# A hybrid attention encoder on one core: the last dilated merge over later slots, the first head's loads and splits reordered, the copies of branch B's values moved into dilated slots

## The chip, the cores and the metric

The kernel runs on one core of one Trainium2 chip. The metric is the device time of one execution in microseconds (us), the median of several runs. Five engines work side by side, each through its own queue in order: TensorE (PE in the profile, PEld for its weight loads), VectorE (DVE), ScalarE (ACT), GpSimd (POOL) and SyncE (SP), which here only issues DMAs.

## The reference

One encoder layer on 1024 positions of width 1024, in float32. What matters here is the attention part, which has two branches on the same normalised input `h`:

```python
proj = h @ w_in
qa, ka, va, qb, kb, vb, ga, gb = split(proj)
oa = mixture_of_dilations(qa, ka, va, rel_bias)      # branch A, 8 heads of 64
ob = neighbourhood_attention_2d(qb, kb, vb, na_rpb)  # branch B, 8 heads of 64
merged = sigmoid(ga) * (oa @ w_branch_dil) + sigmoid(gb) * (ob @ w_branch_na)
x = x + gate1 * (merged @ w_out)
```

Branch A runs three dilated window patterns and merges them per position with weights from their softmax denominators. Branch B is attention over an 8 x 16 neighbourhood on a 16 x 64 grid. A convolutional FFN and a final norm follow.

## The kernel before, in words

Each float32 product is three TensorE products of rounded parts: every operand is split into a high part (an ACT copy into a rounded type) and a low part (a subtraction on POOL or DVE), and high x high, high x low and low x high are summed in PSUM. So each weight tile costs one ACT step and one or two POOL steps before TensorE can use it.

**Stages.** First come the norm and the conditioning, then the values of both branches (`v_wide`), then the queries and keys (`p_products`, the "p stage", lines 500 to 521 and 795 to 850), then attention (lines 852 to 1400), then the branch and output products and the FFN. In the p stage a pair of weight tiles is loaded by `p_load` (L714) and split by `a_operands` (L442 to L461 and the helper's L57 and L61). In this stage a scheduler orders every engine's queue when the kernel is built, from its own estimates of time.

**The copies of branch B's values.** `v_wide` writes vB to `vbc` in DRAM. Four column blocks of it are copied, DRAM to DRAM, to the tensors `vb` from which the heads load (`vb_chunks`, L423, 16 DMAs in all). They are written in the p stage's loop (L829), but the scheduler puts them as early in SP's queue as it finds them ready.

**Attention in slots.** Attention is written as a table: slot 0 to slot 101, and in each slot lists of jobs ("first", "O", "T", "S", "last"). `settle` (L898) opens a slot: it emits the ACT and DVE work that the slot before left. Then come "first", "O" (probabilities times values), "T" (transposes of the probabilities), one step of fill work, "S" (scores) and "last", and one or two more fill steps. Fill work is the gate projection: each step is a triple of 128x512 products (L84 to L86). Small jobs such as splits wait in a side queue (`aside`) and are emitted with the fill steps; `ensure` emits what is not out yet. This order is fixed by hand for PE, ACT, DVE and SP. **POOL's order in attention is not**: the scheduler sets it at build time, by when it believes each step to be ready.

- Dilated heads (`DilHead`): head n starts at slot 8n. It adds a bias part on POOL (L1008), makes `qb` on POOL (L408), splits its values `vv` (ACT L780, POOL L781), and runs scores, softmax (DVE L882, ACT L883), transposes (L1039, L1087), their splits into `th` (ACT L892) and `tl` (DVE L896), and outputs (L1051, L1104).
- Dilated pairs (`DilPair`): two heads share tiles `u1`, `u23`. Their merge is a chain: `spread` reads the denominators back (9 small DMAs), `factors` and `shares` work out the weights on DVE and ACT, `send` writes them to DRAM (`fcs`, 10 DMAs), `load` reads them back broadcast (`fb`, L1183), `weigh` multiplies on POOL (L1188, four times), `merge` adds on POOL (L1197). For the last pair (pr 3, first slot 48) these stand at slots 68 to 81, among the first 2-D heads.
- 2-D heads (`NaHead`): head n starts at slot 64 + 4n. Four column blocks are scored (L1252), softmaxed (DVE L1262, ACT L1264), normalised (reciprocal L1269 on DVE, then one half on POOL and one on DVE, L1272), transposed (L1281) and multiplied (L1294). The values `vv` come by L774 at slot s0 + 2 and are split in three parts (L780, L781).

**The first head** has no slots ahead of it. Its loads, and those that were put beside them (bias and keys of head 1), are issued before the slots start (L854 to L859 and L909), and weight tile 26 of the gate projection is loaded by the fill steps (L1338).

Of the kernel before, what the change touches and what calls it, by code (L numbers as in the profile page):

```python
# [29 lines left out]
def hybrid_encoder(tc, xT, c, w_ada, small, w_in, p1_bias, p23_bias, na_bias, ln2_mult, ident, w_br, w_out,  # L30
# [43 lines left out]
    ahead = {}  # L74
# [320 lines left out]
    def qk_load(head):  # L395
        pr, i = divmod(head, 2)
        a = slice(64 * i, 64 * i + 64)
        qk = [qk2.tile([128, S], FR, name=n) for n in ("qs", "ks", "kl")]
        for y in range(3):
            rows = f(qk[y]).rearrange("(p b) s -> b p s", b=2)  # L400
            for b in range(2):
                sp.dma_start(rows[b], q_scr[pr, 1 + y if y else b, a])
        return qk
# [13 lines left out]
        for j, t0 in ((0, 0), (8, 240)):  # L417
            sp.dma_start(va_b[j, 0:64, cc].rearrange("(r p) n -> r p n", r=4), v4[:, t0:t0 + 16])

    def vb_chunks(cb):  # L420
        t0, n = NA_T0[cb], NA_NC[cb]
        for r in range(4):
            sp.dma_start(vb_s[cb].rearrange("(w t r) n -> r w t n", r=4, t=n)[r],  # L423
                         vb_c[256 * r:256 * r + 256].rearrange("(w t) n -> w t n", t=16)[:, t0:t0 + n])

    STEPS = (("11", "B11"), ("S2", "T2"), ("S1", "T1"), ("S3", "T3"), ("12", "B21"), ("S4", "B22"), ("22", "T4"))
    names = tuple(b for _, b in STEPS)
# [97 lines left out]
    with tc.manual_schedule(engines={e.engine for e in (sp, act, dve, pool, pe)}):  # L525
# [53 lines left out]
        for q in range(4):  # L579
# [16 lines left out]
            last = 6 if q else 5  # L596
# [88 lines left out]
        def v_raw(load, head):  # L685
            vv = sm_pool.tile([128, 16, 128], FR, name="vv", bufs=2)
            load(head, f(vv[:, :, 64:128]))
            return vv

        def dil_bias(head):  # L690
            bt = sm_pool.tile([128, 896], FT, name="bias", bufs=4)
            sp.dma_start(bt[:, 0:512], p1_bias[head])
            sp.dma_start(bt[:, 512:896], p23_bias[head])
            return bt
# [131 lines left out]
    for n in range(len(order)):  # L826
        if n + 2 < len(order):
            raw[n + 2] = p_load(n + 2)
        if 1 <= n < 5:  # L829
            vb_chunks(n - 1)  # L830
        if n + 1 < len(order):
            nxt = prep[1] if n == 0 else a_operands(raw.pop(n + 1), 4, p_home, p_sts[n + 1], spot=p_spot)
            if n:
                next(nxt)
        else:
            ahead.update({t: w_load(w_in[t]) for t in (24, 25)})
            nxt = iter(())
        for j in gens[n] if n < 2 else p_products(n):
            if j in (1, 2, 5):
                next(nxt, None)  # L840
# [12 lines left out]
    with tc.manual_schedule(engines={pool.engine}):  # L853
        qks = {0: qk_load(0)}  # L854
        lnm = sm_pool.tile([128, 384], FT, name="lnm", bufs=1)
        sp.dma_start(lnm, ln2_mult)
        biases = {0: dil_bias(0)}
        values = {0: v_raw(va_load, 0)}
        biases[1] = dil_bias(1)  # L859
        pool.tensor_tensor(biases[0][:, 512:896], biases[0][:, 512:896], lnm, OP.add)  # L860
        q_blocks(qks[0])

# [43 lines left out]
        turned.clear()  # L906
        scored.clear()

    qks[1] = qk_load(1)  # L909
    side, second, count, credit = collections.deque(), collections.deque(), [0, 0], [0]  # L910

    def aside(ns, one=lambda: None, two=lambda: None):
# [64 lines left out]
    class DilHead:  # L977
        def __init__(self, pair, pr, i, s0, u, st):
            self.pair = pair
            self.pr, self.i, self.u, self.st, self.head = pr, i, u, st, 2 * pr + i  # L980
            self.a = slice(64 * i, 64 * i + 64)
            self.P, self.tt, self.po = {}, {}, {}
            if self.head > 1:
                at(s0 - 5, "first", self.load)
                at(s0 - 7, "first", lambda: qks.update({self.head: qk_load(self.head)}))
            if self.head:
                at(s0 - 3, "first", self.load_v)
                at(s0 - 2, "first", self.prepare)
                at(s0 - 1, "first", lambda: q_blocks(qks[self.head]))
            at(s0, "first", self.values)  # L990
            for n in range(4):
                at(s0 + n, "S", self.far_scores, n)
                at(s0 + n + 2, "T", self.far_turn, n)
                at(s0 + n + 4, "O", self.far_out, n)
                at(s0 + n + 4, "S", self.near_scores, n)
                for js in (((0, 1),), ((2, 3),), ((4, 5),), ((6, 7), (8,)))[n]:
                    at(s0 + n + 6 + (js == (8,)), "T", self.near_turn, js)
                    at(s0 + n + 8 + (js == (8,)), "O", self.near_out, js)
# [10 lines left out]

        def values(self):  # L1010
            self.bt, self.vv = biases.pop(self.head), values.pop(self.head)
            for n in range(0, 16, 8):
                self.mark = aside(600, lambda n=n: v_tile(self.vv, ((128, slice(n, n + 8)),)))

# [96 lines left out]
    class DilPair:  # L1111
        def __init__(self, pr):
            self.pr, s0 = pr, 16 * pr
            at(s0, "first", self.begin) if pr else self.begin()
            for i in range(2):
                DilHead(self, pr, i, s0 + 8 * i, lambda: self.u, lambda: self.st)
            at(s0 + 17, "T", self.turn)
            at(s0 + 20, "first", self.spread)
            at(s0 + 22, "last", self.factors)
            at(s0 + 23, "last", self.shares)  # L1120
            at(s0 + 24, "first", self.send)
            for z in range(2):
                at(s0 + 26, "first", self.load, 1, z)
            for n, g, z in ((28, 1, 0), (29, 1, 1), (31, 0, 0), (32, 0, 1)):
                at(s0 + n, "last", self.weigh, g, z)
            at(s0 + 33, "first", self.merge)

        def begin(self):
            self.u = [at_pool.tile([128, S], FT, name=n) for n in ("u1", "u23")]
# [72 lines left out]
    class NaHead:  # L1202
        def __init__(self, head, s0):
            self.head, self.i = head, head % 2
            self.a = slice(64 * self.i, 64 * self.i + 64)
            self.P, self.t3, self.bt = {}, {}, {}
            at(57 if head == 0 else s0 - 4, "first", lambda: qks.update({8 + head: qk_load(8 + head)}))
            at(s0, "first", self.begin)
            at(s0 + 2, "first", self.load)
            at(s0 + 4, "last", self.prepare)  # L1210
            for n, cb in enumerate((0, 3, 1, 2)):
                at(s0 + n - 2, "first", self.bias, cb)
                at(s0 + n, "S", self.scores, cb)
                at(s0 + n + 2, "first", self.normalise, cb)
            for n, pair in enumerate(((0, 3), (1, 2))):
                s = s0 + 4 + 2 * n
                for y in range(3):
                    at(s + (y == 2), "T", self.turn, pair, y)
                at(s + 3, "O", self.out, pair)
# [1 line left out]
        def begin(self):  # L1221
            self.st = at_pool.tile([128, 2, 8], FT, name="stb", bufs=3)

        def load(self):
            if self.i == 0:
                oTs[self.head // 2] = (gspool.tile([128, S], FT, name="last", bufs=1) if self.head == 6 else
                                       at_pool.tile([128, S], FT, name=("u1", "u23")[self.head // 2 % 2]))
            self.vv = v_raw(vb_load, self.head)

        def prepare(self):  # L1230
# [81 lines left out]
    def fill_steps():  # L1312
        w, raw = first_w, {1: ahead.pop(25)}
        w_mark = 0
        marks, held = [0, 0], []

        def out(p, n, hf):
            g = gspool.tile([128, 512], FT, name="gs")
            act.activation(g, p, AF.Copy)
            if now[0] < LAST:  # L1320
                later(1, lambda: sp.dma_start(g_scr[n][:, halves[hf]], g))
            else:
                act.dma_start(g_scr[n][:, halves[hf]], g)

        def release():
            while held:
                args = held.pop()
                marks.append(aside(600, lambda: out(*args)))
        for n in range(16):
            ensure(w_mark)  # L1330
            if n < 15:
                w_next = [wpool.tile([128, KT, 128], FR, name=x_) for x_ in ("whi", "wlo")]
                w_mark = side_split(raw.pop(n + 1), *w_next)
            if n < 14:
                raw[n + 2] = w_load(w_in[26 + n])
            elif n == 14:
                w_raw[0] = w_load(w_br[0])
            for hf in range(2):  # L1338
                ensure(marks[2 * n + hf])
                p = ps_g.tile([128, 512], FT, name="pj")  # L1340
                for k in range(KT):
                    product(p, w, lambda k: h[hf, k], ks=[k])
                    if k == 1:
                        release()
                    if k == KT - 1:
                        held.append((p, n, hf))
                        if n == 15 and hf:
                            release()
                    yield
            w = w_next  # L1350
# [3 lines left out]
        DilPair(pr)  # L1354
    for head in range(8):
        NaHead(head, 64 + 4 * head)
    steps = fill_steps()

    def fill(n, asides=True):
# [758 lines left out]
```

## Time and profile before

| What | Value |
|---|---|
| Time, median of 3 runs | 1481.3 us (1480.17 to 1482.05) |
| The profiled execution | 1483.17 us, of which the span from first to last instruction is 1481.3 us |
| PE busy | 1448.3 us, 98% of the span |
| POOL, DVE, ACT busy | 58%, 64%, 53% of the span |
| PE's granted clock, mean | 0.994 of full speed |

The page gives shares of a span that has stages with quite different limits. TensorE is busy nearly throughout, so what is left to win or lose lies in short places where it waits, or where its clock is lower; these are read from the windows (busy time and granted clock by stretch) and from the timeline, which gives the idle time ahead of an instruction in brackets with what ended it.

### The profile page before, as it was taken

Reading aid. Unit: us, or ns where it says so; the run is one execution under the profiler, and the core shown is the slowest. Engines: PE = TensorE matmul, PEld = TensorE weight load, DVE = VectorE, ACT = ScalarE, POOL = GpSimd, SP = SyncE. Lnnn points to the kernel's source line nnn. Section 1 sums busy time; section 2 is a strip of 40 time slices with the busy share of each in tenths; the row PEclk is TensorE's granted clock in tenths of the full one; section 3 lists DMA queues with packets and bytes.
Section 4 is the critical chain, followed back from the end, with each engine's and each line's share of the span. In section 5 each row is a group of like instructions: output and inputs, shape, how many; then the busy total and the mean of one; then the engine's idle time right before and its main releaser. Section 6 shows DMA issues by size and latency. Waiting matters only on the chain.

```text
span 1481.3 us, 21309 instructions
## 1 busy us (share of the span) xinstructions
PE 1448.3 (98%) x7308; PEld 1224.1 (83%) x7308; DVE 952.1 (64%) x1793; ACT 792.3 (53%) x1479; POOL 858.5 (58%) x706
## 2 busy tenths in 40 slices
PE   9999999999999989999999999999999999999998
PEld 8887788788888878888888878888888888887787
DVE  7696544255555756666516897666666667787865
ACT  6634543277777657653346554444444447475542
POOL 4155775434554566512267678766666676988712
PEclk9999999999999999999999999999999999999999
DMA  9598354654765788477644313222222233542313
GB/s 368 206 349 293 124 185 178 216 156 138 209 189 169 228 259 276 146 271 255 196 155 138 108 52 134 85 86 86 86 85 82 69 132 128 199 149 65 110 37 114
DMA packets 130516, 241.14 MB, mean 163 GB/s; under 512 B 47812, under 2 KB 60740, under 8 KB 130372
## 3 DMA queue, kind: packets, MB, share of 16 engines
q1 hardware_dynamic: 121176, 219.00, 45.2%
q10 hardware_dynamic: 9232, 20.78, 3.8%
q8 instruction: 58, 0.95, 0.3%
q14 instruction: 50, 0.41, 0.1%
HBM read 185.60 MB, written 59.90 MB: 166 GB/s over the span
## 4 chain that ended last, share of the span: by engine, by line
PE 76%; DVE 7%; DMA 5%; POOL 4%; ACT 3%; issue 3%; SPq 1%; ACTq 0%; DVEq 0%; POOLq 0%
PE pj L496 14%; PE pj L497 14%; PE pj L498 14%; PE pj L84 8%; PE pj L85 7%; PE pj L86 7%; PE O L1294 1%; PE O L1104 1%; PE O L1051 1%; PE T L1039 1%; PE T L1281 1%; PE T L1087 1%; DVE op L1648 1%; PE S L1252 1%; POOL wlo L61 1%
## 5 line engine op out<-in xcount | busy, mean ns | idle before, releaser
L61 POOL TENSOR_TENSOR wlo<-wraw,whi 128x512 fp32r<-128x512 f32 (+1 forms) x90 | 114.1, 1289 | 129.3 <-ACT whi L57 127.5
L496 PE MATMUL pj<-op,wsh 128*128 128x512 f32 x408 | 158.7, 390 | 1.6 <-ACT wsh L57 1.6
L497 PE MATMUL pj<-op,wsh 128*128 128x512 f32 x408 | 158.9, 390 | 0.5 <-DVE op L1537 0.5
L498 PE MATMUL pj<-op,wsl 128*128 128x512 f32 x408 | 157.6, 390 | 0.0
L61 POOL TENSOR_TENSOR wsl<-big,wsh 128x512 fp32r<-128x512 f32 (+1 forms) x86 | 111.7, 1321 | 44.4 <-ACT wsh L57 39.4
L84 PE MATMUL pj<-h,whi 128*128 128x512 f32 x272 | 116.8, 430 | 0.0
L86 PE MATMUL pj<-h,wlo 128*128 128x512 f32 x272 | 107.7, 396 | 0.0
L85 PE MATMUL pj<-h,whi 128*128 128x512 f32 x272 | 107.7, 396 | 0.0
L1747 DVE SCALAR_TENSOR_TENSOR big<-pj,sm,big 128x512 f32<-128x512 f32 (+2 forms) x183 | 94.9, 563 | 16.5 <-ACT big L1741 15.5
L882 DVE CUSTOM_DVE_ANT_0 P<-S,bias 128x256 f32<-128x256 f32 x128 | 49.1, 421 | 68.2 <-PE S L1024 39.5
L496 PEld LDWEIGHTS pj<-op,wsh 128*128 128x128 f32 x408 | 76.6, 188 | 18.3 <-ACT wsh L57 2.5
L496 PE MATMUL pj<-op,whi 128*128 128x512 f32 x232 | 90.8, 391 | 0.3 <-ACT wc L502 0.3
L497 PE MATMUL pj<-op,whi 128*128 128x512 f32 x232 | 90.6, 391 | 0.2 <-DVE op L1567 0.2
L497 PEld LDWEIGHTS pj<-op,wsh 128*128 128x128 f32 x408 | 76.6, 188 | 16.8 <-DVE op L1537 0.9
L498 PE MATMUL pj<-op,wlo 128*128 128x512 f32 x232 | 90.4, 390 | 0.0
L61 POOL TENSOR_TENSOR wsl<-wraw,wsh 128x384 fp32r<-128x384 f32 (+1 forms) x46 | 56.7, 1254 | 57.3 <-ACT wsh L57 53.0
L498 PEld LDWEIGHTS pj<-op,wsl 128*128 128x128 f32 x408 | 76.7, 188 | 15.9 <-POOL wsl L61 0.2
L883 ACT ACTIVATE P<-P,st 128x256 f32<-128x256 f32 x128 | 64.0, 502 | 38.2 <-DVE st L882 37.9
L896 DVE TENSOR_TENSOR tl<-T,th 128x512 fp32r<-128x512 f32 (+3 forms) x120 | 76.0, 648 | 11.5 <-ACT th L892 11.5
L57 ACT ACTIVATE whi<-wraw 128x1024 fp32r<-128x1024 f32 (+2 forms) x48 | 47.5, 993 | 58.3 <-PE pj L85 33.5
L1741 ACT ACTIVATE big<-pj,sm 128x512 f32<-128x512 f32 x61 | 47.0, 773 | 54.2 <-DVE pj L517 32.2
L517 DVE TENSOR_TENSOR pj<-pj,wc 128x512 f32<-128x512 f32 x40 | 27.8, 695 | 71.9 <-PE pj L498 71.9
(478 smaller groups left out, 4566.0 us busy)
## 6 DMA issues: line engine op xcount, KB each, us to landing
wada<-w_ada SPq DMA_DIRECT2D x31, 512.0 KB
qks<-qs ACTq DMA_DIRECT2D x28, 512.0 KB
wraw<-w_in SPq DMA_DIRECT2D x24, 512.0 KB
big<-w_up SPq DMA_DIRECT2D x22, 512.0 KB
wraw<-w_up SPq DMA_DIRECT2D x22, 512.0 KB
big<-as SPq DMA_DIRECT2D x22, 512.0 KB
as<-big SPq DMA_DIRECT2D x21, 512.0 KB
qs<-qks SPq DMA_DIRECT2D x32, 256.0 KB
```

What stands on the lines that cost most here:

```text
L57: act.activation(hi, raw, AF.Copy)
L61: lo_eng.tensor_tensor(lo[:, i:i + step], raw[:, i:i + step], f(hi)[:, i:i + step], OP.subtract)
L84: pe.matmul(psum, whi[:, k0 + k], mhi, start=k == 0, stop=False)
L85: pe.matmul(psum, whi[:, k0 + k], mlo, start=False, stop=False)
L86: pe.matmul(psum, wlo[:, k0 + k], mhi, start=False, stop=k == n - 1)
L496: pe.matmul(psum, whi[:, k], bhi, start=j < 4 and k == 0, stop=False, skip_group_check=True)
L497: pe.matmul(psum, whi[:, k], blo, start=False, stop=False, skip_group_check=True)
L498: pe.matmul(psum, wlo[:, k], bhi, start=False, stop=k == n - 1, skip_group_check=True)
L882: dve.tensor_tensor_reduce(pp, d, bias, -1.0, BIG, OP.add, OP.min, mi)
L883: act.activation(pp, pp, AF.Exp, bias=mi, scale=-1.0, accum_out=li)
L896: dve.tensor_tensor(tt[1][:m, :n], pt[:m, :n], f(tt[0])[:m, :n], OP.subtract)
L1747: dve.scalar_tensor_tensor(y[:, dst], src, wt, y[:, dst], OP.mult, OP.add)
```

## The change

Four edits, all of them in which order work is issued; no arithmetic changes.

1. The 16 copies of vB are no longer written in the p stage. Each is a job of its own at slots 10, 12, ... 40.
2. The first head: weight tile 26 is loaded ahead of the first head's values. The bias and the keys of head 1 are no longer loaded before the slots start but by head 1's own jobs (slots 3 and 1). The splits of head 0's values, which were emitted in slot 0, are emitted in slot 2.
3. The last pair's merge steps move from slots 68, 70, 71, 72, 74, 76, 77, 79, 80, 81 to 70, 72, 73, 74, 76, 79, 80, 83, 84, 85.
4. A 2-D head's values are split from slot s0 + 5 "first" on (it was s0 + 4 "last"), and its output tile is taken at s0 + 6 (it was s0 + 2).

```diff
-    def vb_chunks(cb):
+    def vb_chunk(cb, r):
         t0, n = NA_T0[cb], NA_NC[cb]
-        for r in range(4):
-            sp.dma_start(vb_s[cb]..., vb_c[256 * r:256 * r + 256]...)
+        sp.dma_start(vb_s[cb]..., vb_c[256 * r:256 * r + 256]...)
...
-        if 1 <= n < 5:
-            vb_chunks(n - 1)
...
         biases = {0: dil_bias(0)}
+        ahead[26] = w_load(w_in[26])
         values = {0: v_raw(va_load, 0)}
-        biases[1] = dil_bias(1)
...
-    qks[1] = qk_load(1)
...
-            if self.head > 1:
+            if self.head:
                 at(s0 - 5, "first", self.load)
                 at(s0 - 7, "first", lambda: qks.update({self.head: qk_load(self.head)}))
...
             at(s0, "first", self.values)
+            at(s0 if self.head else 2, "first", self.split_values)
...
-            at(s0 + 20, "first", self.spread)
...
+            steps = (22, 24, 25, 26, 28, (31, 32, 35, 36), 37) if pr == 3 else (20, 22, 23, 24, 26, (28, 29, 31, 32), 33)
+            at(s0 + steps[0], "first", self.spread)
...
-            at(s0 + 4, "last", self.prepare)
+            at(s0 + 6, "first", self.output)
+            at(s0 + 5, "first", self.prepare)
...
-                raw[n + 2] = w_load(w_in[26 + n])
+                raw[n + 2] = ahead.pop(26) if n == 0 else w_load(w_in[26 + n])
...
+    for n in range(16):
+        at(10 + 2 * n, "last", vb_chunk, (0, 3, 1, 2)[n // 4], n % 4)
```

Three places show what this does to the queues. Line numbers of the changed kernel differ a little: L423 is L422, L714 is L713, L780 and L781 are L779 and L780, L883 is L880, L892 is L889, L956 and L957 are L952 and L953, L1272 is L1275, L1319 is L1322.

The first is SP's queue at the start of the p stage. `wraw` and `xr` are weight tiles, `vb<-vbc` the copies. Before:

```order
L423 DMA vb<-vbc 96x1x512
L423 DMA vb<-vbc 128x1x512 x2
L423 DMA vb<-vbc 96x1x512
L714 DMA wraw<-w_in 128x1024 x2
L423 DMA vb<-vbc 96x1x512
L423 DMA vb<-vbc 128x1x512 x2
L423 DMA vb<-vbc 96x1x512
L316 DMA vbc<-vs 128x512
L423 DMA vb<-vbc 96x1x512
L423 DMA vb<-vbc 128x1x512
L714 DMA xr<-w_in 128x1024 x2
```

And with the change, from the same place:

```order
L713 DMA wraw<-w_in 128x1024 x2
L316 DMA vbc<-vs 128x512
L713 DMA xr<-w_in 128x1024 x2
L316 DMA vbc<-vs 128x512
L713 DMA xr<-w_in 128x1024 x2
```

Ten copies that stood ahead of the first two `xr` loads are gone from there. The scheduler has reordered TensorE's queue in this stage too: between the first product with the new tile's high part and the first with its low part `wlo` there stood 18 products with `op` and `kl`, and there stand 9 now.

The second is ACT's queue at the start of the slots. `vv` is the split of head 0's values, `P,st` the exponentials, `th` the split of a transpose, `whi<-wraw` the split of tile 26. Before:

```order
L1319 ACTIVATE gs<-pj 128x512
L780 ACTIVATE vv<-vv 128x8x64 x2
L883 ACTIVATE P,st<-P,st 128x256 x4
L956 ACTIVATE whi<-wraw 128x512
L892 ACTIVATE th<-T 128x512
```

With the change:

```order
L1322 ACTIVATE gs<-pj 128x512
L880 ACTIVATE P,st<-P,st 128x256 x4
L779 ACTIVATE vv<-vv 128x8x64 x2
L889 ACTIVATE th<-T 128x512
L880 ACTIVATE P,st<-P,st 128x256 x2
L952 ACTIVATE whi<-wraw 128x512 x2
```

The first exponentials stand ahead of the value splits, and the first `th` stands ahead of the split of tile 26.

The third is POOL's queue around the first two `weigh` steps of the last pair (`u<-u,fb`). `P<-P,stb` is a half of a normalisation, `vv` the low part of a value split. Before:

```order
L1272 TENSOR_SCALAR P<-P,stb 128x288
L957 TENSOR_TENSOR wlo<-wraw,whi 128x512 x2
L1188 TENSOR_TENSOR u_4512<-u_4512,fb 128x512
L1272 TENSOR_SCALAR P<-P,stb 128x288
L1188 TENSOR_TENSOR u_4512<-u_4512,fb 128x512
L1272 TENSOR_SCALAR P<-P,stb 128x384
L781 TENSOR_TENSOR vv<-vv 96x4x64
```

With the change:

```order
L1275 TENSOR_SCALAR P<-P,stb 128x288 x2
L953 TENSOR_TENSOR wlo<-wraw,whi 128x512 x2
L1275 TENSOR_SCALAR P<-P,stb 128x384
L1188 TENSOR_TENSOR u_4512<-u_4512,fb 128x512 x2
L780 TENSOR_TENSOR vv<-vv 96x4x64
L1275 TENSOR_SCALAR P<-P,stb 128x384
```

Two normalisations of the 2-D head that starts at slot 72 now stand ahead of the `weigh` steps (those of slots 75 and 76), and both `weigh` steps stand in a row ahead of its last one (slot 77).

More of the change, by code (lines that the diff above doesn't have):

```diff
@@ L418, in va_chunks @@
             sp.dma_start(va_b[j, 0:64, cc].rearrange("(r p) n -> r p n", r=4), v4[:, t0:t0 + 16])
-    def vb_chunks(cb):
+    def vb_chunk(cb, r):
         t0, n = NA_T0[cb], NA_NC[cb]
-        for r in range(4):
-            sp.dma_start(vb_s[cb].rearrange("(w t r) n -> r w t n", r=4, t=n)[r],
-                         vb_c[256 * r:256 * r + 256].rearrange("(w t) n -> w t n", t=16)[:, t0:t0 + n])
+        sp.dma_start(vb_s[cb].rearrange("(w t r) n -> r w t n", r=4, t=n)[r],
+                     vb_c[256 * r:256 * r + 256].rearrange("(w t) n -> w t n", t=16)[:, t0:t0 + n])
     STEPS = (("11", "B11"), ("S2", "T2"), ("S1", "T1"), ("S3", "T3"), ("12", "B21"), ("S4", "B22"), ("22", "T4"))
@@ L1011, in values, with split_values @@
             self.bt, self.vv = biases.pop(self.head), values.pop(self.head)
+        def split_values(self):
             for n in range(0, 16, 8):
@@ L1117, in __init__ @@
             at(s0 + 17, "T", self.turn)
-            at(s0 + 20, "first", self.spread)
-            at(s0 + 22, "last", self.factors)
-            at(s0 + 23, "last", self.shares)
-            at(s0 + 24, "first", self.send)
+            steps = (22, 24, 25, 26, 28, (31, 32, 35, 36), 37) if pr == 3 else (20, 22, 23, 24, 26, (28, 29, 31, 32), 33)
+            at(s0 + steps[0], "first", self.spread)
+            at(s0 + steps[1], "last", self.factors)
+            at(s0 + steps[2], "last", self.shares)
+            at(s0 + steps[3], "first", self.send)
             for z in range(2):
-                at(s0 + 26, "first", self.load, 1, z)
-            for n, g, z in ((28, 1, 0), (29, 1, 1), (31, 0, 0), (32, 0, 1)):
+                at(s0 + steps[4], "first", self.load, 1, z)
+            for n, g, z in zip(steps[5], (1, 1, 0, 0), (0, 1, 0, 1)):
                 at(s0 + n, "last", self.weigh, g, z)
-            at(s0 + 33, "first", self.merge)
+            at(s0 + steps[6], "first", self.merge)
         def begin(self):
@@ L1222, in begin, with output @@
             self.st = at_pool.tile([128, 2, 8], FT, name="stb", bufs=3)
-        def load(self):
+        def output(self):
             if self.i == 0:
@@ L1227, in load @@
                                        at_pool.tile([128, S], FT, name=("u1", "u23")[self.head // 2 % 2]))
+        def load(self):
             self.vv = v_raw(vb_load, self.head)
```

## The prediction

> **What bounds the kernel now.** I read the page first. TensorE is busy for nearly the whole span and no other engine passes two thirds of it:
>
> ```profile
> span 1481.3 us, 21309 instructions
> PE 1448.3 (98%) x7308; PEld 1224.1 (83%) x7308; DVE 952.1 (64%) x1793; ACT 792.3 (53%) x1479; POOL 858.5 (58%) x706
> ```
>
> TensorE's work is the same before and after the change, so only its idle time (33 us in all) and the time that it loses at a lower clock can move. Next the windows, which give by stretch the busy time of PE, PEld, DVE, ACT and POOL, the granted clock, the share of DMA and GB/s. Of the stretches that the change touches, three have PE idle, and a fourth, which the copies enter, has not:
>
> ```profile
> 125.00:150.00 25.00, 23.28 (x108) 18.37 (x106) 17.19 (x27) 16.43 (x30) 7.63 (x7) 1.00 0.84 279
> 275.00:300.00 25.00, 20.44 (x102) 16.48 (x101) 6.36 (x21) 7.51 (x20) 13.19 (x14) 1.00 0.81 257
> 525.00:550.00 25.00, 20.25 (x112) 17.78 (x111) 12.50 (x39) 13.66 (x36) 14.64 (x14) 0.86 0.90 274
> 300.00:425.00 125.00, 124.25 (x784) 110.41 (x783) 71.77 (x243) 94.31 (x260) 54.66 (x51) 0.99 0.55 161
> ```
>
> The first is the start of the p stage, the second the start of attention, the third slots 74 to 79. In each I then read the timeline of PE and of the engine that it waits for.
>
> **Edit 1, at the start of the p stage.** TensorE waits twice for the first new weight tile, first for its high part and then for its low part:
>
> ```profile
> 144.76 0.50 PE L496 MATMUL pj<-h,whi 128*128 128x512 f32 x1 [1.31 <-ACT whi L57]
> 145.33 0.40 PE L496 MATMUL pj<-op,kl 128*128 128x512 f32 x1
> 149.20 0.39 PE L498 MATMUL pj<-op,kl 128*128 128x512 f32 x1
> 151.27 0.50 PE L498 MATMUL pj<-h,wlo 128*128 128x512 f32 x1 [1.68 <-POOL wlo L61]
> ```
> ```profile
> 131.11 2.66 SPq L423 DMA_DIRECT2D vb<-vbc  x4
> 136.70 0.33 SPq L316 DMA_DIRECT2D vbc<-vs  x1
> 138.42 1.01 SPq L714 DMA_DIRECT2D xr<-w_in  x2
> 143.65 1.06 ACT L57 ACTIVATE whi<-xr 128x1024 fp32r<-128x1024 f32 x1 [1.29 <-DMA xr<-w_in]
> 146.08 1.29 POOL L442 TENSOR_TENSOR ks<-xr 128x512 f32<-128x512 f32 x1 [17.21 <-DMA xr<-w_in]
> 149.95 2.51 POOL L61 TENSOR_TENSOR wlo<-xr,whi 128x512 fp32r<-128x512 f32 x2
> ```
>
> Both together are 1.31 + 1.68 = 2.99 us. The first `xr` landed 143.65 − 138.42 = 5.2 us after its issue, the second 7.7, while the copies kept the DMA engines at a share of 0.84; then POOL needs 5.1 us from the second landing to the end of the first `wlo` step (146.08 to 149.95 + 1.25). Without copies `xr` is issued right behind `vbc<-vs`, at some 137.1, 1.3 us earlier, and I take the shorter 5.2 us for both: landed at about 142.4, `wlo` ready at 147.5. The wait for `whi` is gone by this. But TensorE also comes earlier: without the first wait it starts at 143.45, does two products with `whi` (0.57 us), and then has 9 products with `op`, `kl` in place of 18, each (149.20 − 145.33)/17 = 0.228 us. So it wants `wlo` at 143.45 + 0.57 + 2.05 = 146.1 and waits 1.4. Gain 2.99 − 1.4 = about 1.5; ends 0 (a landing 1.5 us later than I take it) and 3.0 (all of it).
>
> The Trainium skill, "DMA: Bandwidth & Descriptors", section "Anatomy of one DMA — SWDGE (gpsimd) path", fits 2.0 us plus the bytes over 436 kB/us; for 512 KB that is an estimate of 3.2 us, against the 5.2 and 7.7 us of these rows, and by it the gain would be the full 3.0. The rows decide, since other transfers still share the engines.
>
> The 16 copies come back at slots 10 to 40, one in every second slot. Four issues take SP 2.66 us, so each 0.67. In the fourth window above DMA is busy by 0.55 and PE idles only 0.75 us in 125. The loads of a head stand 5 to 7 slots ahead of its use, and that distance is the cover. I take 0 and weigh the contrary below.
>
> **Edit 2, at the start of attention.** The first transposes wait for the exponentials (L883), the first outputs for `th` (L892), and two stretches behind run at a lower clock:
>
> ```profile
> 290.35 0.33 PE L1039 MATMUL T<-idt,P 128*128 128x128 f32 x1 [1.56 <-ACT P L883]
> 298.78 0.36 PE L1051 MATMUL O<-th,vv 128*128 128x256 f32 x1 [2.55 <-ACT th L892]
> ```
> ```profile
> 287.19 0.42 DVE L882 CUSTOM_DVE_ANT_0 P<-S,bias 128x256 f32<-128x256 f32 x1 [7.50 <-POOL bias L860]
> 289.18 0.63 ACT L780 ACTIVATE vv<-vv 128x512 fp32r<-128x512 f32 x1 [0.96 <-DMA vv<-v]
> 290.39 2.52 POOL L781 TENSOR_TENSOR vv<-vv 128x512 fp32r<-128x512 f32 x2
> 291.74 0.33 SPq L65 DMA_DIRECT2D wraw<-w_in  x1
> 297.52 0.63 ACT L956 ACTIVATE whi<-wraw 128x512 fp32r<-128x512 f32 x1 [5.75 <-DMA wraw<-w_in]
> 298.06 0.58 ACT L892 ACTIVATE th<-T 128x512 fp32r<-128x512 f32 x1
> ```
> ```profile
> 300.00:302.00 2.00, 2.00 (x10) 1.71 (x8) 0.73 (x3) 2.00 (x8) 1.28 (x1) 0.52 0.27 82
> 302.00:304.00 2.00, 2.00 (x11) 1.83 (x10) 0.66 (x3) 0.76 (x3) 0.00 (x0) 0.63 0.92 225
> ```
>
> ACT's queue explains both waits. The exponentials stand behind the `vv` splits, which wait for their load; `th` stands behind the split of tile 26, which was issued at 291.74 and landed 5.8 us later. The idle time is 25.00 − 20.44 = 4.56 us of the second window; at the clocks 0.52 and 0.63 two stretches of 2 us lose 0.96 + 0.74 = 1.70 us of full-speed work. In all 6.26. With the change the exponentials need only DVE's 287.19 + 0.42, and take until about 288.8, where the transposes are wanted (290.35 − 1.56): a wait of some 0.2 stays. Tile 26, issued ahead of `vv`, is there long before its split. What is late next is `vv`: 512 KB more stand ahead of it, at the 257 GB/s of that window 2 us, so it comes at 289.6 to 291.2, and ACT's two `vv` splits (0.63 each) end by 291.8, `th` at 292.4; the `vv` low parts on POOL (2.52) end at about 294.4, when the outputs are due (296.2 less the 1.56 that is gone, so about 294.7). That is just in time. Gain 6.0; ends 6.3 and, if the outputs wait for `vv`, 3.
>
> The Trainium skill, "TensorE: Matmul & The Clock Gate", section "Part 1: The HAM clock gate (the "warmup" mystery)", says that the clock halves after an idle window of about 3.4 us. By it a wait of 2.55 us would keep the clock and edit 2 would win 1.7 less; the rows above show 0.52 of full speed behind just this wait, so I count the 1.7.
>
> **Edit 3, in the 2-D slots.** At slot 76 TensorE's second transposes wait 4.41 us for a normalisation on POOL, which stands behind a `weigh` (L1188) that waits for `fb`:
>
> ```profile
> 523.42 0.60 PE L1281 MATMUL T<-idt,P 128*128 128x128 f32 x4
> ...
> 531.99 0.60 PE L1281 MATMUL T<-idt,P 128*96 128x128 f32 x4
> 537.00 1.09 PE L1281 MATMUL T<-idt,P 128*96 128x128 f32 x4 [4.41 <-POOL P L1272]
> 546.03 0.60 PE L1281 MATMUL T<-idt,P 128*128 128x128 f32 x4
> ```
> ```profile
> 469.39 2.53 SPq L1183 DMA_DIRECT2D fb<-fcs  x4
> 526.16 2.57 SPq L1183 DMA_DIRECT2D fb<-fcs  x4
> 475.56 1.30 POOL L1188 TENSOR_TENSOR u<-u,fb 128x512 f32<-128x512 f32 x1 [8.46 <-DMA fb<-fcs]
> 534.70 1.26 POOL L1188 TENSOR_TENSOR u<-u,fb 128x512 f32<-128x512 f32 x1 [6.64 <-DMA fb<-fcs]
> 538.16 1.24 POOL L1272 TENSOR_SCALAR P<-P,stb 128x384 f32<-128x384 f32 x1
> 623.87 0.72 POOL L781 TENSOR_TENSOR vv<-vv 96x256 fp32r<-96x256 f32 x1
> ```
> ```profile
> 537.00:540.00 3.00, 3.00 (x11) 2.68 (x12) 0.02 (x1) 1.59 (x3) 3.00 (x3) 0.50 1.03 379
> 540.00:543.00 3.00, 3.00 (x15) 2.71 (x14) 2.96 (x8) 1.45 (x5) 2.32 (x4) 0.60 1.02 362
> ```
>
> Two stretches of 3 us at 0.50 and 0.60 lose 1.5 + 1.2 = 2.7, so the place costs 4.41 + 2.7 = 7.1 us. With the change the first two `weigh` steps stand ahead of a part of the `vv` split and of the normalisation of slot 77, for which the second transposes of slot 78 wait. From the first transposes of slot 76 to these are 546.03 − 531.99 − 7.1 + 0.4 = 7.3 us (0.4 for slot 78's first four, which overlap their successors). Before them POOL must do two `weigh` (1.26 to 1.30 each), the split (0.72) and the normalisation (1.24): 4.6 with issue. So `fb` may take 7.3 − 4.6 = 2.7 us counted from slot 76. From issue to first `weigh` it takes 6.2 us in the row of 469 and 8.5 in that of 526. With the change no group of `qs`, `ks`, `kl` and no weight tile stands right ahead of it in SP's queue, only `vv` and two `bias`, so I take somewhat less than the shorter row, 5.7. `fb` is asked for in slot 76 at the earliest place, and SP, which was 2.7 us behind the first transposes of slot 74 (523.42 to 526.16) right after issuing ten `fcs`, now has one slot more behind these, so it should be about 1 us ahead of PE. The wait is then 5.7 − 1 − 2.7 = 2.0 us, which I count without a loss of clock (1.68 us left it at 1.00 in the first stretch, 2.55 halved it in the second). The last two `weigh` steps, one slot apart, may cost 0.5. Gain 7.1 − 2.0 − 0.5 = about 4.5; upper end 7.1, lower end under the first rival.
>
> **Edit 4** puts the splits one job later and the output tile four slots later. The order has one visible cost: the third part of the last head's split comes out only when its output needs it, which can show its POOL step (0.72); I take 0.5 lost.
>
> **Sum:** 1.5 + 6.0 + 4.5 − 0.5 = 11.5 us. The profiled execution took 1483.17 us, 1.9 above the median of 1481.3; 1483.2 − 11.5 = 1471.7 for an execution like it, and 1469.8, rounded 1470, against the median.
>
> **Rivals.**
>
> *The stall of edit 3 only moves.* `fb` takes 8.5 us as at 526, since DMA in slots 74 to 79 is busy by 0.90, and is issued no earlier than slot 76 begins: 8.5 − 2.7 = 5.8 us idle, and with the same 2.7 of clock 8.5 in all, 1.4 more than now. Then 1.5 + 6.0 − 1.4 − 0.5 = 5.6, and 1475.7. For it speaks that SP was behind in slot 74; against it, the shorter queue ahead. Chance 0.21.
>
> *Half of edit 2 comes back.* `vv` lands behind tile 26 so late that outputs wait as they do now, with the clock: 3 in place of 6, and 1472.8. For it speaks that the slack worked out above is only 0.3 us; against it, that the loads of head 1, which shared the 257 GB/s, are gone from there. Chance 0.11.
>
> *Slower: the copies stall the dilated slots.* Each copy moves some 0.23 MB out of DRAM and into it, on the queue that brings the heads' queries, keys, biases and values. If each made TensorE wait 1.2 us, 16 waits would cost 19.2, and the time were 1489. It decides from 11.5/16 = 0.7 us a copy on. Against it stand the DMA share of 0.55 and the idle 0.75 us of the fourth window; for it, that the stretch of before shows no copy there, so its price is unknown. Chance 0.04.
>
> *It hardly shows.* The first two rivals together, and a `wlo` that lands as late as now: 0 + 3.0 − 1.4 − 0.5 = 1.1, and 1480.2. Chance 0.05.
>
> **How the numbers follow.** The forecast has 0.59, and is the likeliest: 1470. The low end takes each term at its best, 3.0 + 6.3 + 7.1 = 16.4, so 1465. The high end holds the first rival at 1475.7 and something of its joint case with the second (1478.7): 1477. What is left out is "hardly shows" and "slower", 0.09, and a little at the edges. A measurement of this kernel tells about 0.2%, 3 us, from no change, so faster is below 1478.3: the forecast and the first two rivals, 0.91; same 0.05; slower 0.04.
>
> **What the profile after would show.** Right: `xr` issued at about 137 and no wait for `whi`; in the second stretch no wait above 0.5 us, and a clock of 1.00 behind it; at slot 76 no wait, at slot 78 one of about 2 us for POOL; 300 to 425 as long as now. Wrong: outputs that wait for `vv` or `th` in slot 4; a wait above 4 us for `P` in slot 78 with a clock near 0.5 behind it; PE idle in the dilated slots ended by loads. I should be wrong as a whole if these three places had gained and the time had not, since then PE would be late elsewhere.

## The result and the profile after

| | Before | Changed |
|---|---|---|
| Median, first comparison (4 runs each) | 1481.7 us | 1471.3 us |
| Ratio, 95% interval | | 0.9927 (0.991 to 0.9944) |
| Profiled execution, its span | 1483.17 us, 1481.3 us | 1471.7 us, 1469.7 us |

The forecast was 1470 us; the changed kernel took 1471.3, some 10 us less than before. The page of the changed kernel:

```profile
span 1469.7 us, 21289 instructions
PE 1443.2 (98%) x7308; PEld 1221.1 (83%) x7308; DVE 952.6 (65%) x1793; ACT 793.5 (54%) x1479; POOL 860.9 (59%) x706
```

PE's idle time falls from 33.0 to 26.5 us (span less busy), and its busy time by 5.1 us for the same 7308 products. About 3.4 us of this is clock won back: in the kernel before, the clock stood at 0.50 for 3.4 us from 300.1 us on and for 6.8 us from 535.6 on, and in the changed kernel only for 3.4 us from 558.5 on (half of the 6.8 us that are gone). The rest is not traced. The windows, in the columns of the prediction, one stretch added:

```profile
125.00:150.00 25.00, 24.34 (x114) 19.58 (x113) 18.44 (x29) 17.57 (x31) 10.06 (x9) 1.00 0.53 187
275.00:300.00 25.00, 24.88 (x135) 21.14 (x134) 9.46 (x31) 12.58 (x34) 13.31 (x14) 1.00 0.84 250
525.00:550.00 25.00, 22.75 (x151) 20.31 (x150) 16.26 (x52) 18.33 (x48) 17.13 (x16) 1.00 0.88 282
550.00:575.00 25.00, 23.12 (x142) 20.56 (x141) 16.79 (x51) 15.58 (x43) 16.00 (x16) 0.93 0.89 255
300.00:425.00 125.00, 124.14 (x793) 110.29 (x792) 72.63 (x246) 94.32 (x259) 58.35 (x55) 1.00 0.68 204
```

The start of attention (second row) idles for 0.12 us where it idled for 4.56. The dilated slots (last row) carry the copies, with DMA busy by 0.68 for 0.55, and PE idles there 0.86 us for 0.75. The fourth row got worse. In the kernel before, which is some 7 us less far at the same time, it read

```profile
550.00:575.00 25.00, 24.11 (x159) 21.58 (x158) 17.49 (x54) 18.87 (x53) 18.14 (x17) 1.00 0.88 277
```

so PE idled 0.9 us at full clock there; now it idles 1.9 us and runs at 0.93. The timeline of PE gives the waits above 0.6 us between 90 and 600 us, without one of 0.92 at slot 70 that stands there before and after:

```profile
101.77 0.47 PE L309 MATMUL pv<-vwl,h 128*128 128x512 f32 x1 [2.17 <-DVE vwl L61]
148.90 0.50 PE L497 MATMUL pj<-h,wlo 128*128 128x512 f32 x1 [0.66 <-POOL wlo L61]
518.37 0.63 PE L1284 MATMUL T<-idt,P 128*128 128x128 f32 x4 [1.54 <-DVE stb L1272]
535.35 0.66 PE L1284 MATMUL T<-idt,P 128*128 128x128 f32 x4 [1.81 <-DVE u L1310]
556.84 0.40 PE L1297 MATMUL O<-th,vv 96*128 96x256 f32 x1 [1.55 <-POOL vv L780]
```

The first of them is in the values' stage, where the order of no engine was changed. The wait at 535 (slot 78) is put down to a DVE step that had ended; POOL's normalisation, below, ends right at it.

To see what is the change's and what is chance, I cut each execution at three places that all kernels have: where the first transposes of attention were due (start less wait), a transpose at 344.80 us before (337.82 after), and from the 0.92 us wait of slot 70 (504.51; 497.60) to the first output of slot 101 (629.90; 621.44). These are the pieces, in us, of every kernel run here (a second row is a second profile):

| Kernel | Waits of 95 to 105 and 140 to 155 us | Transposes due at | To the transpose in slot 18 | Slots 70 to 101 | From there to the end |
|---|---|---|---|---|---|
| before | 0 + 2.99 | 288.8 | 56.0 | 125.4 | 851.4 |
| changed | 2.17 + 0.66 | 288.4 | 49.4 | 123.8 | 848.3 |
| changed, again | 0.17 + 0.68 | 286.9 | 49.1 | 121.6 | 848.5 |
| edit 1 alone | 0 + 0.66 | 286.3 | 55.4 | 124.7 | 849.4 |
| edit 2 alone | 0 + 3.08 | 288.7 | 49.1 | 122.4 | 852.3 |
| edit 3 alone | 1.11 + 1.00 | 288.5 | 57.2 | 120.4 | 851.6 |
| edit 4 alone | 1.29 + 0.84 | 288.2 | 56.4 | 125.4 | 848.8 |
| edit 2, splits only | 0 + 2.48 | 289.0 | 55.0 | 125.6 | 853.0 |
| edit 2, loads only | 0 + 3.46 | 289.5 | 54.0 | 123.8 | 851.4 |
| without edit 4 | 0 + 0.81 | 286.0 | 49.1 | 120.2 | 849.4 |
| without edit 4, again | 1.65 + 0.65 | 288.1 | 49.0 | 120.3 | 851.6 |
| merge later | 1.22 + 0.84 | 287.5 | 49.4 | 119.2 | 852.1 |
| merge later, again | 0 + 0.85 | 286.4 | 49.1 | 118.7 | 848.7 |
| merge earlier | 1.31 + 1.16 | 288.0 | 49.1 | 120.5 | 851.5 |

The last column varies by 4.7 us and follows no edit (two profiles of one kernel, the merge later, differ by over 3 us in it): I take it as chance, as is the wait at 101 us, which stands in one profile of a kernel and not in the other. The stretch between the second and third cut (slots 18 to 70) is left out of the table: it lasts 159.65 to 159.71 us without the copies and 159.78 to 159.88 with them.

### The profile page after: what moved, and what is told of

Its sections match the earlier page's. It is cut to its first block, busy times and chain, and to the rows that moved or that the text cites. A ratio compares the mean times of both kernels' runs of the same rounds, so it can differ in the third digit from the quotient of the medians.

```text
span 1469.7 us, 21289 instructions
## 1 busy us (share of the span) xinstructions
PE 1443.2 (98%) x7308; PEld 1221.1 (83%) x7308; DVE 952.6 (65%) x1793; ACT 793.5 (54%) x1479; POOL 860.9 (59%) x706
## 4 chain that ended last, share of the span: by engine, by line
PE 51%; DVE 3%; ACT 1%; DMA 1%; issue 1%; POOL 0%; SPq 0%; DVEq 0%; ACTq 0%; POOLq 0%
PE pj L495 12%; PE pj L496 12%; PE pj L497 12%; PE pj L84 5%; PE pj L85 5%; PE pj L86 5%; DMA wraw<-w_down 1%; DVE big L1752 0%; DVE op L1653 0%; POOL wsl L61 0%; DVE wlo L61 0%; ACT wsh L57 0%; PE pcol L108 0%; ACT op L1652 0%; DVE x L1824 0%
## 5 line engine op out<-in xcount | busy, mean ns | idle before, releaser
L880 ACT ACTIVATE P<-P,st 128x256 f32<-128x256 f32 x128 | 64.1, 502 | 41.2 <-DVE st L879 41.0
```

Source lines behind the costliest of these rows:

```text
L880: act.activation(pp, pp, AF.Exp, bias=mi, scale=-1.0, accum_out=li)
```

## The experiments

**The four edits one by one**, each put alone into the kernel before. Edit 1 is the diff's `vb_chunk` part:

> Edit 1 alone (the 16 copies of vB at slots 10 to 40). My theory: the two waits at the start of the p stage, 2.99 us before, fall to about 0.7, and the copies cost nothing in the dilated slots (300 to 425 as long as before), so about 1479.0 against 1481.3, ratio 0.9984. Rival, the copies stall the dilated slots: PE idle there above 3 us, ended by loads, and a ratio of 1.000 or more.

Measured: 1480.0 against 1481.5, ratio 0.9986 (0.9973 to 0.9999). The waits at the start of the p stage are 0.66 us, and the copies cost 0.1 us in slots 18 to 70. The rival falls: its stall of 3 us is not there.

Edit 2, the first head's part of the diff:

> Edit 2 alone (tile 26 ahead of the values, head 1's loads later, splits of head 0 in slot 2). My theory: the waits of slots 0 to 4 (4.56 us) and the lower clock behind them (1.7 us) go, 6.3 to 6.7 us, so about 1475, ratio 0.9957. Rival, the values land so late behind tile 26 that the outputs wait with the clock as before: half of it, about 1478, ratio 0.998.

Measured: 1473.8, ratio 0.9945 (0.9925 to 0.9965); the second cut comes 6.9 us sooner after the first. The values do not hold it: in the changed kernel, whose order there is the same, ACT's queue (timeline) reads

```profile
289.14 0.49 ACT L880 ACTIVATE P<-P,st 128x256 f32<-128x256 f32 x1
...
289.95 0.63 ACT L779 ACTIVATE vv<-vv 128x512 fp32r<-128x512 f32 x1 [0.23 <-DMA vv<-v]
291.19 0.63 ACT L779 ACTIVATE vv<-vv 128x512 fp32r<-128x512 f32 x1 [0.60 <-DMA vv<-v]
291.72 0.58 ACT L889 ACTIVATE th<-T 128x512 fp32r<-128x512 f32 x1
...
293.19 1.14 ACT L952 ACTIVATE whi<-wraw 128x512 fp32r<-128x512 f32 x2
```

so the splits wait for their load 0.83 us in all, and POOL's low parts end at 290.66 + 2.55 = 293.2, ahead of the outputs at 294.0:

```profile
290.66 2.55 POOL L780 TENSOR_TENSOR vv<-vv 128x512 fp32r<-128x512 f32 x2 [0.24 <-ACT vv L779]
```

Edit 3, the `steps` of the last pair:

> Edit 3 alone (the last pair's merge over later slots). My theory: 7.1 us of slot 76 go, 1.5 to 2 us come back at slot 78 for fb and about 1 us at slot 74; the loss of 3.2 us that the changed kernel shows at slot 83 (outputs that wait for the third part of the value split, and the clock behind it) does not come, since it belongs to edit 4: a gain of 4, so about 1477.3, ratio 0.9973. Rival, that loss belongs to edit 3, by the weigh steps of slots 83 and 84: a gain of 1 to 2, about 1480, ratio 0.999.

Measured: 1478.0, ratio 0.9975 (0.9959 to 0.9991). Slots 70 to 101 take 5.0 us less. The waits in them:

```profile
525.32 0.63 PE L1282 MATMUL T<-idt,P 128*128 128x128 f32 x4 [0.75 <-DVE stb L1270]
542.06 0.66 PE L1282 MATMUL T<-idt,P 128*128 128x128 f32 x4 [1.57 <-POOL P L1273]
567.07 0.61 PE L1282 MATMUL T<-idt,P 128*96 128x128 f32 x4 [1.14 <-DVE stb L1270]
```

No output waits for a value split, and no lower clock follows: with edit 3 alone the loss at slot 83 isn't there, and by this the rival falls. The time alone would not decide it, since its interval holds the theory's 0.9973 and the rival's 0.999. The last of the three waits stands at slot 84.

Edit 4, `prepare` at s0 + 5 "first" and `output` at s0 + 6:

> Edit 4 alone (the 2-D heads' value splits one job later, the output tile later). My theory: the wait of 4.4 us at slot 76 stays, since POOL's weigh still stands ahead of the normalisation, and the time is the same within 1.5 us, ratio 0.999 to 1.001. Rival, the later splits free the normalisations of POOL: the wait at slot 76 falls below 3 us and the ratio to 0.997.

Measured: 1482.9, ratio 1.0007 (0.9995 to 1.002): no gain, and the wait of slot 76 stands at 4.12 us. The four ratios multiplied give 0.9913, inside the change's interval.

**Edit 2 taken apart.** The splits alone are `at(s0 if self.head else 2, "first", self.split_values)`, the loads alone all the rest of edit 2.

> Of edit 2 only the later splits: head 0's values are split in slot 2, all loads stand as before, tile 26 is still loaded by the fill steps. My theory: the order in ACT's queue is what cost the time, so both waits (1.7 and 2.8 us) and the lower clock go without any load being moved: 6 us or more, about 1475, ratio 0.996. Rival, the late landing of tile 26 costs it: only the wait for the exponentials goes, 1.7 us, and th or tile 26 itself holds PE with a lower clock behind: about 1479.5, ratio 0.9985.

> Of edit 2 only the loads: tile 26 ahead of the values, head 1's bias and keys later, splits in slot 0 as before. My theory: ACT's exponentials still stand behind the value splits, and the values land later, so the first transposes wait longer (3 us for 1.6); the wait of 2.8 us for th goes: a gain of 1 to 3, about 1479, ratio 0.9985. Rival, tile 26 is what matters: gain of 4.5 or more with the clock, ratio 0.997 or less.

Measured: 1481.1, ratio 0.9995 (0.9982 to 1.0007), and 1480.5, ratio 0.9997 (0.9986 to 1.0008): in the times neither half can be told from no change, and both together give 0.9945. In the profiles, by the second cut, the halves win 1.0 and 2.0 us of the 6.9. My theory, that the order in ACT's queue is what cost the time, fell for the splits, and for the loads it was right on the wait but hoped for too much. With the splits alone, ACT's queue and PE's are

```profile
297.75 1.15 ACT L956 ACTIVATE whi<-wraw 128x512 fp32r<-128x512 f32 x2 [5.15 <-DMA wraw<-w_in]
...
299.29 0.59 ACT L892 ACTIVATE th<-T 128x512 fp32r<-128x512 f32 x1
```
```profile
299.93 0.58 PE L1054 MATMUL O<-th,vv 128*128 128x256 f32 x1 [2.45 <-ACT th L892]
```
```profile
300.00:302.00 2.00, 1.85 (x7) 1.56 (x8) 1.92 (x6) 2.00 (x8) 0.96 (x1) 0.50 0.71 194
302.00:304.00 2.00, 2.00 (x8) 1.71 (x7) 0.74 (x2) 1.50 (x4) 0.00 (x0) 0.50 0.97 203
304.00:306.00 2.00, 2.00 (x9) 1.71 (x8) 1.32 (x5) 0.85 (x3) 0.00 (x0) 0.50 0.04 4
```

The exponentials come in time and the first `th` too, but the split of tile 26 has only moved behind them, and the next `th` behind it: one `th` later, PE waits 2.45 us as before, with a lower clock behind it as before. That this lasts 6.8 us here and 3.4 in the kernel before is not the edit's doing: with edit 3 alone, which leaves these queues as they were, it lasted 6.8 us too (from 298.3 us on). With 3.4 us, this half would have won about 2.7 us (an estimate: 1.0 and half of 3.4). With the loads alone the first transposes wait for ACT:

```profile
290.30 0.63 ACT L780 ACTIVATE vv<-vv 128x512 fp32r<-128x512 f32 x1 [5.97 <-DMA vv<-v]
291.53 0.63 ACT L780 ACTIVATE vv<-vv 128x512 fp32r<-128x512 f32 x1 [0.59 <-DMA vv<-v]
```
```profile
292.70 1.39 PE L1038 MATMUL T<-idt,P 128*128 128x128 f32 x4 [3.25 <-ACT P L883]
```

Tile 26 no longer holds `th`, but it has pushed the values back, and the exponentials still stand behind those. ACT's queue has two gates in a row; taking out one lets the other have most of the time.

**The last merge.** Three kernels carry edits 1 to 3 without edit 4, with other slots for the last pair:

```diff
 no_edit4:      steps = (22, 24, 25, 26, 28, (31, 32, 35, 36), 37)
 merge_later:   steps = (22, 24, 25, 26, 29, (32, 33, 36, 37), 38)
 merge_earlier: steps = (21, 23, 24, 25, 27, (31, 32, 35, 36), 37)
```

> The changed kernel without edit 4 (value splits from the slot before again, output tile taken early). My theory: the wait of 1.55 us at slot 83 for the third part of a value split, and the clock lost behind it (1.7 us), are edit 4's and go, so 2 to 3 us faster than the changed kernel: about 1468.5, ratio 0.9912. Rival, they belong to the weigh steps of slots 83 and 84 in any order: the same as the changed kernel, ratio 0.9927.

> The same without edit 4, and with the last merge's loads and weigh steps one slot later still (load 77, weigh 80, 81, 84, 85, merge 86), by which POOL does both first weigh steps behind the normalisation of slot 77 in place of ahead of it. My theory: the wait of 1.6 us at slot 78 was for POOL, and goes: 1 to 2 us less than without edit 4, about 1467, ratio 0.990. Rival, the wait only moves by one slot again, to the normalisation that then stands behind the weigh steps: no gain, or a wait of 2 us and more with a lower clock at slot 79 or 80.

Measured: without edit 4 1470.9, ratio 0.9932 (0.9915 to 0.9949), the merge later 1467.1, ratio 0.9907 (0.989 to 0.9923). The first is no faster than the change by its interval, so the 2 to 3 us of my theory did not show, though its trace lacks the wait at slot 83; it has one of 1.39 us at slot 84 instead, for a normalisation behind a `weigh`. So all were run beside the changed kernel on one chip:

> The changed kernel itself, to be compared with the two below on one chip. My theory: 1471, ratio 0.9927, with the waits of 1.5 us at slot 74, 1.8 at slot 78 and 1.6 at slot 83 again at their places, and the wait of 2.2 us that its first trace shows at 101.8 us, in a part whose order the change does not touch, not always there (0 to 2.4 us). Rival: that wait is the change's and stands there again at 2 us.

> Without edit 4, beside the changed kernel on one chip. My theory: 2 to 3 us faster than that (the wait of slot 83 and the clock behind it), ratio about 0.991. Rival: within 1 us of it.

> Without edit 4 and with the last merge's loads and weigh steps one slot later, beside the two above on one chip. My theory: another 1 to 1.5 us faster than without edit 4, about 1467, ratio 0.990. Rival: the same as without edit 4.

> Without edit 4, and with the first five steps of the last merge one slot earlier than in the change (69, 71, 72, 73, load at 75; weigh steps where the change has them). By this POOL's order has both first weigh steps ahead of the normalisation of slot 76. My theory: fb comes 3.7 us earlier, so the weigh steps are done before POOL is needed, and the wait at slot 78 falls from 1.1 to below 0.5: 0.5 to 1 us faster than without edit 4. Rival: weigh waits for fb ahead of both normalisations, as before the change, and the wait at slot 78 grows above 2 us, with a lower clock: 2 us slower than without edit 4.

Measured: the changed kernel 1471.4, ratio 0.9925 (0.9907 to 0.9942); without edit 4 1469.6, ratio 0.9912 (0.9893 to 0.9931); merge later 1467.9, ratio 0.9905 (0.9888 to 0.9923); merge earlier 1472.0, ratio 0.9932 (0.9915 to 0.9948). Over the ten runs of each, the medians are 1471.4 for the change, 1470.4 without edit 4, 1467.4 with the merge later. Edit 4 costs 1.3 to 3.6 us in slots 70 to 101 by the profiles (1.7 of the 3.6 is the lower clock); in the times its 1 us isn't clear of noise. The merge later wins another 1.0 to 1.7 us there by the profiles; its 3 us in the times are not clear of noise against the kernel without edit 4, by the intervals above. The changed kernel's second profile has the same places, smaller at two, and no lower clock behind them:

```profile
516.82 0.63 PE L1284 MATMUL T<-idt,P 128*128 128x128 f32 x4 [1.53 <-DVE stb L1272]
533.05 0.66 PE L1284 MATMUL T<-idt,P 128*128 128x128 f32 x4 [1.07 <-POOL P L1275]
553.76 0.39 PE L1297 MATMUL O<-th,vv 96*128 96x256 f32 x1 [0.80 <-POOL vv L780]
```

The merge one slot later has no wait above 0.4 us at slot 78: POOL has done slot 77's normalisation before it comes to the first `weigh`, and nobody waits for that.

```profile
529.22 1.41 POOL L1272 TENSOR_SCALAR P<-P,stb 128x384 f32<-128x384 f32 x1
532.33 1.08 POOL L1272 TENSOR_SCALAR P<-P,stb 128x288 f32<-128x288 f32 x1 [1.69 <-DVE stb L1269]
534.87 1.30 POOL L1188 TENSOR_TENSOR u<-u,fb 128x512 f32<-128x512 f32 x1 [1.45 <-DMA fb<-fcs]
```

Here a `weigh` still waits 1.45 us for `fb`, at no cost. The merge earlier went the rival's way in part: both `weigh` steps wait for `fb` (3.02 and 0.80 us) ahead of both normalisations, and the wait at slot 78 grew to 1.82 us, without a lower clock. Its median is 2.4 us above that without edit 4, as the rival had it, but its slots 70 to 101 take only 0.2 to 0.3 us more, since the wait at slot 84 is shorter (0.52 us for 1.39 and 1.79); where the rest comes from stays open. The version with edits 1 to 3 and the merge later is the fastest that ran: about 4 us less than the change, 14 less than before.

## Why the prediction was right, step by step

**Edit 1** (forecast 1.5). `xr` landed about 5 us after its issue, as taken (138.68 to 143.67), and `wlo` came 5.1 us behind that; the wait for `whi` is gone, the one for `wlo` is 0.66 where I had 1.4. The issue came at about 137, as forecast, in the second profile (136.89); the first is later by about as much as PE waits at 101 us. By the cut at the first transposes, edit 1 wins 1.9 to 2.8 us against before's 288.8 in the executions without the wait at 101 us (286.0 to 286.9: four of them), and 0.4 to 1.3 where that wait has made PE late anyway (287.5 to 288.4: four). So the term held as a mean: the eight executions with edit 1 average 287.2, the six without it 288.8. Like with like it is two terms: among the executions without the wait at 101 us edit 1 wins 2.6 us (four average 286.4, four without it 289.0), among those with it 0.4 (four average 288.0, two without it 288.4). A late PE finds its tile nearly there: the waits of the p stage are 2.5 to 3.5 us without edit 1, but 0.8 to 1.0 without it where the wait at 101 us came first. That 1.5 fits the mean is luck of the mix. The copies cost nothing that counts, as I took it. The Trainium skill's fit ("DMA: Bandwidth & Descriptors", "Anatomy of one DMA — SWDGE (gpsimd) path") is for DMAs that GpSimd issues, and gave an estimate of 3.2 us; this load is issued by SP, and the rows show 5.0 even with the copies gone.

**Edit 2** (forecast 6.0): 6.6 to 6.9 by the second cut. Both mechanisms were right, each link with its time: exponentials from 287.6, values split at 290.0 and 291.2, outputs just behind POOL's low parts. The prediction treated the two waits as separate sums, though; the halves show that they are one chain, and that removing either alone gives little.

**Edits 3 and 4** (forecast 4.5 − 0.5 = 4.0): 1.6 and 3.8 in the two profiles. The 7.1 us of slot 76 did go, and the wait at slot 78 came, for the cause and nearly of the size I had (2.0; measured 1.81 and 1.07):

```profile
523.69 2.54 SPq L1183 DMA_DIRECT2D fb<-fcs  x4
```
```profile
529.63 1.29 POOL L1188 TENSOR_TENSOR u<-u,fb 128x512 f32<-128x512 f32 x1 [1.78 <-DMA fb<-fcs]
531.97 1.29 POOL L1188 TENSOR_TENSOR u<-u,fb 128x512 f32<-128x512 f32 x1 [1.06 <-DMA fb<-fcs]
533.22 0.72 POOL L780 TENSOR_TENSOR vv<-vv 96x256 fp32r<-96x256 f32 x1
533.93 1.37 POOL L1275 TENSOR_SCALAR P<-P,stb 128x384 f32<-128x384 f32 x1
```

`fb` took 5.9 us to the first `weigh` (I had 5.7), and the second `weigh` waited another 1.06, which I had not. Against that SP was 2.3 us ahead of slot 76's first transposes (526.00), not 1. So the size of 2.0 came out by two errors that cancel (5.9 − 2.3 − 2.7 + 1.06 is 2.0 again). The reason I gave for that 1 us was wrong: loads stand two slots behind the `fcs` issues before and after, not one more.

What was mis-sized are the prices of the new neighbours: 0.5 for the last two `weigh` steps and 0.5 for edit 4. Together they cost two waits and, once, clock. At slot 83 an output waits for the third part of a value split (1.55 and 0.80 us), which stands on POOL behind the third `weigh`, and that waits for `fb`; without edit 4 the split stands ahead of it. In the changed kernel:

```profile
553.67 1.30 POOL L1188 TENSOR_TENSOR u<-u,fb 128x512 f32<-128x512 f32 x1 [2.26 <-DMA fb<-fcs]
554.94 1.02 POOL L1275 TENSOR_SCALAR P<-P,stb 128x288 f32<-128x288 f32 x1
555.91 0.88 POOL L780 TENSOR_TENSOR vv<-vv 96x256 fp32r<-96x256 f32 x1
```

At slot 74 the wait is 1.54 us where it was 0.32. There DVE has two short steps that last far longer than usual:

```profile
512.90 1.53 DVE L1275 TENSOR_SCALAR P<-P,stb 128x384 f32<-128x384 f32 x1
...
515.25 1.61 DVE L1166 TENSOR_TENSOR fa<-fa,fl 64x32 f32<-64x32 f32 x2
```
```profile
512.91 0.74 POOL L780 TENSOR_TENSOR vv<-vv 96x256 fp32r<-96x256 f32 x1 [2.37 <-DVE stb L1272]
513.63 1.25 POOL L1275 TENSOR_SCALAR P<-P,stb 128x384 f32<-128x384 f32 x1
514.84 1.99 POOL L780 TENSOR_TENSOR vv<-vv 128x512 fp32r<-128x512 f32 x2
```

At the same place of the kernel before, the first takes 0.42 us and the two of L1166 0.28. Both lie beside POOL steps, the two of L1166 end with one (516.86 and 516.83), and in the changed kernel's second profile they are 1.52 and 1.61 again. In the kernel with the merge earlier, which has no edit 4, the two of L1166 come beside POOL's value splits by another way, and last as long as these:

```profile
509.94 2.70 DVE L1166 TENSOR_TENSOR fa<-fa,fl 64x32 f32<-64x32 f32 x2
```
```profile
509.90 2.69 POOL L780 TENSOR_TENSOR vv<-vv 96x256 fp32r<-96x256 f32 x3
```

The Trainium skill, "SBUF — State Buffer", section "Who interferes with whom", says that a DVE step with two inputs in SBUF contends with a POOL step that reads SBUF, and calls the port pair they share an exclusive lock; the rows of L1166 agree. The first step ends in the middle of a POOL step (at 514.43, while that step runs from 513.63 to 514.88), so why it lasts longer stays open. Edit 3 put the merge's small DVE steps, and edit 4 POOL's value splits, into the same slot: with edit 3 alone the two of L1166 take 0.28 us and the wait is 0.75. That the lock causes it was not tried by itself.

**The sum** of the profiled executions was 11.6 us (forecast 11.5), and partly by luck: 0.4 up to the first transposes, 6.6, −0.1 in the dilated slots, 1.6 in slots 70 to 101, and 3.1 behind them, where no instruction was moved and the column varies by itself. In the times, 10.4 us in the first comparison; the terms' means (1.6, 6.7, 2.7) make 11.0.

## What to carry to other kernels

When an in-order queue holds two steps that wait for different loads, cost them as one chain: removing the first gate buys little while the second stands right behind it, and each half measured alone looks worthless. A step that waits for a slow transfer is best put behind the last step in its queue that somebody needs soon; moving it a slot later (in the experiment, behind slot 77's normalisation) was worth more than loading earlier. Cut the profiles of several executions at common instructions before crediting a term: here 3 us of an 11.6 us difference stood in a part that nothing had touched. And compare executions that are alike ahead of the edit: a wait upstream that comes and goes changed what edit 1 was worth from 2.6 to 0.4 us.

## What the runs showed of the hardware

Between the first and the last 10 us or so, the clock was lowered for 3.4 or 6.8 us at a time, to 0.50, but not by the length of a wait alone. With edit 2 alone it stayed at 1.00 through a wait of 3.46 us at slot 76, while 1.55 us at slot 83 were enough in the changed kernel:

```profile
529.27 0.64 PE L1283 MATMUL T<-idt,P 128*96 128x128 f32 x4 [3.46 <-POOL P L1274]
```

The traces show why, in part. Their record of the clock changes only on a grid. In the kernel before it changes at 300.07, 303.48, 535.59, 542.42 and 1474.26 us, and these lie 1, 68, 2 and 273 times 3.4133 us apart. So it is in all 14 traces, to 0.002 us, counted from the first entry of the record (at 4.0 to 7.0 us, 6.52 here). So I cut the time into cells of 3.41 us on this grid and took PE's idle time by cell. A cell of the kernel before, two of the changed kernel and two of edit 2 alone (columns: stretch, us, PE busy, granted clock, DMA share, GB/s):

```profile
296.66:300.07 3.41, 1.01 (x6) 1.00 0.59 238
```
```profile
555.09:558.50 3.41, 1.86 (x15) 1.00 0.56 99
558.50:561.91 3.41, 3.41 (x10) 0.50 0.93 343
```
```profile
523.92:527.34 3.42, 1.89 (x11) 1.00 0.99 223
527.34:530.75 3.41, 1.48 (x10) 1.00 1.05 235
```

PE idled 2.4 us in the first, and the clock fell at its end (300.07). It idled 1.55 us in the second, and the third ran at 0.50. The wait of 3.46 us lies across the last two, which idled 1.53 and 1.93 us, and the clock stayed. Over all 14 traces, among the cells at full clock up to 1455 us, the fall came behind all 11 that idled 2.1 to 3.3 us, behind one of the 15 that idled 1.5 to 1.95 us, and behind none that idled less. What decides between 1.5 and 1.95 us the traces do not show.

The Trainium skill ("TensorE: Matmul & The Clock Gate", "Part 1: The HAM clock gate (the "warmup" mystery)") speaks of free-running windows of about 3.4 us and of a fall after an idle one. The grid and the lengths agree; that 1.55 us, or 2.1, of a cell were enough does not agree with a whole idle window. In a forecast the place of the grid is not known (the first entries differ by up to 2.9 us), so the clock behind a wait of 1.5 to 3.5 us is a chance, of 1.7 or 3.4 us; a wait above some 4.2 us leaves 2.1 us in one cell wherever it lies, and by these counts would always cost it (an estimate).
